# Nine buffers for the preparation of the right operands in a hybrid attention and gated-linear-attention block

## The chip, the cores and the metric

The kernel runs on one core of a Trainium2 chip. The core has a matrix engine (TensorE, PE in the profile; PEld are its weight loads), a vector engine (VectorE, DVE), a scalar engine (ScalarE, ACT), GpSimd (POOL) and SyncE (SP), which here issues every transfer of data. The engines run side by side. Each works through its own list of instructions in order and waits where an instruction needs a result that isn't there yet. Sixteen DMA engines move the data that SP's instructions ask for. The metric is the device time of one execution in microseconds.

## What is computed

One decoder layer over 2048 tokens of 1024 features, all in float32. The normalized input goes through one wide projection. A part of its columns feeds sliding-window attention (16 heads, window 128), another a gated linear attention (GLA, 4 heads, in chunks of 64 tokens). The outputs of both, each times its own gate, go through the output projection; a per-layer embedding, times a gate of the residual stream, is added.

```python
u = rmsnorm(h, norm_mix[i])
z = u @ w_in[i]                                   # 1024 x 5392
aq, ak, av, gq, gk, gv, g_low, za, zg = jnp.split(z, offsets, axis=-1)
...
y = jnp.concatenate([y_att * jax.nn.silu(za), y_gla * jax.nn.silu(zg)], axis=-1) @ w_out[i]
h = h + y                                         # w_out: 2048 x 1024
gate = jax.nn.sigmoid(rmsnorm(h, ple_norm[i]) @ w_ple_gate[i])   # 1024 x 1024
h = h + gate * (p[i] @ w_ple_proj[i])
```

## The kernel before

**Precision.** Every float32 operand of a large product is split into a rounded part (float32r) and the rest, and three products of these are added up (`gemm`, lines 85 to 87). The rounding is done by ACT, the subtraction that gives the rest by DVE or POOL.

**First phase.** The tokens are worked in two halves of eight tiles of 128. In each half come section A (keys, values and low-rank gates), then for each of the four GLA heads `v_block`, `qk_block`, `gla_prep` and `gla_tile`, and behind them the attention groups (`za_block`, `att_tile`). Results go to DRAM as yts (stores yts<-oy from attention, line 480, and yts<-oyg from GLA, line 587). In the first half `load_w` reads a piece of w_in into a buffer raw, splits it into wh and wl and stores both to DRAM (wd); in the second half it loads wh and wl from there.

**Second phase.** Three products of 1024 x 1024 matrices (the two halves of w_out, then w_ple_gate) are done in a seven-product scheme. Its right operands T0 to T6 are sums and differences of the blocks of the weight matrix, split as above. `products` uses them in the order ORDER = (0, 4, 1, 6, 5, 2, 3), for one or two pairs of token tiles at a time.

**Right operands.** They are prepared in the second half of the first phase by the generator `right_operands` in 48 pieces (3 matrices, 4 row blocks, 4 column blocks). A piece loads four 128 x 128 blocks of the weights (tile rb, line 605); DVE forms four differences of them (tile tm, `diff`, line 104); then, once for three blocks of rb and once for tm, ACT rounds into a tile th (line 620), POOL subtracts in place (line 621), and SP stores both parts to DRAM, td0 to td2 (line 623). These four tiles of a piece, and the raw pieces of `load_w`, share one pool, rawp, of three buffers of 2176 bytes per partition. `tick` advances the generator between the tiles of the main work; where it yields it gives its turn away. The loads of the next piece stand at the end of a piece.

**Order.** The program is built by a framework that schedules the instructions of each engine at build time and picks the buffer of each tile. So a yield sets when a piece is offered, and what stands where in an engine's list is seen in the order of the built program.

**Between the phases.** When the last group of the second half begins, the pool kvp (keys, values and attention scratch) is closed and T0 and T4 are loaded in its space (pool tpr, `load_T`, line 122). The other five are loaded when the first phase's pools are closed (pool tpb), behind the loads of the second phase's first left operands (y<-yts) and residuals (xt<-in_x).

Of the kernel before, what the change touches and what calls it, by code (L numbers as in the profile page):

```python
# [11 lines left out]
F32R = mybir.dt.float32r  # L12
# [7 lines left out]
P = 128  # L20
# [18 lines left out]
def hybrid_block_kernel(  # L39
# [5 lines left out]
    nc = tc.nc  # L45
# [44 lines left out]
    p2p = {}  # L90
# [12 lines left out]
    def diff(eng, o, i0, i1):  # L103
        eng.tensor_tensor(o, i0, i1, op=ALU.subtract)  # L104
# [9 lines left out]
    ORDER = (0, 4, 1, 6, 5, 2, 3)  # L114
    srcs = [w_out[0:D, :], w_out[D:2 * D, :], w_ple_gate]

    def load_T(ps_, which, T):
        for i in which:
            T[i] = p2p["tpr" if i in ORDER[:2] else "tpb"].tile(
                [P, 2, 4, 512], F32R, name=f"T{i}", tag="T", bufs=2 if i in ORDER[:2] else 5)  # L120
            for k in range(4):
                nc.sync.dma_start(T[i][:, :, k, :].bitcast(F32), tds[ps_][:, i, :, k, :])

# [2 lines left out]
    with ExitStack() as p1:  # L126
        kvs = p1.enter_context(ExitStack())
        kvp = kvs.enter_context(tc.tile_pool(name="kvp", bufs=1, side="right"))
        rawp = p1.enter_context(tc.tile_pool(name="rawp", bufs=3))
        wps = [p1.enter_context(tc.tile_pool(name=f"wp{i}", bufs=1)) for i in range(2)]  # L130
        up = p1.enter_context(tc.tile_pool(name="up", bufs=1))
        c1 = p1.enter_context(tc.tile_pool(name="c1", bufs=1))
# [175 lines left out]
        def tick():  # L308
            for c in list(chains):
                if next(c, True):  # L310
                    chains.remove(c)

        def spawn(c):
            chains.append(c)
# [12 lines left out]
        def u_norm(half, lt):  # L327
            t = half * HT + lt
            xt = u_load(half, lt)
            junk = w2("junk", BF16, (P, 1024))  # L330
            ss = small.tile([P, 1], F32, name="ss", tag="ss", bufs=4)
            act.activation(junk, xt, AF.Square, accum_out=ss)
            rs = rms_scale(ss, D)
            xts[t] = (xt, rs)

        def u_scale(half, lt):
            xt, rs = xts[half * HT + lt]
            for sl in ((slice(0, 512), slice(512, 1024)) if half + lt == 0 else (slice(0, 1024),)):
                dve.scalar_tensor_tensor(xt[:, sl], xt[:, sl], rs, nm[:, sl], op0=ALU.mult, op1=ALU.mult)
# [14 lines left out]
        def carry_kv():  # L354
            act.activation(kT[:, :, :, 0:P], kT[:, :, :, HT * P:(HT + 1) * P], AF.Copy)
            act.activation(vs[:, 0], vs[:, HT], AF.Copy)
# [232 lines left out]
        def run_chain(c):  # L589
            next(c)  # L590
            tick()
            spawn(c)


        def right_operands():
            units = [(ps_, k, c) for ps_ in range(3) for k in range(4) for c in range(4)]

            def piece(name, dtype=F32):
                return rawp.tile([P, 2 * SW], dtype, name=name, tag="raw")[:, 0:512].rearrange("p (b n) -> p b n", b=4)

            def load(ps_, k, c):
                r = piece("rb")

                for i, (kk, a) in enumerate(((0, 1), (0, 0), (1, 0), (1, 1))):
                    nc.sync.dma_start(r[:, i], srcs[ps_][(k + 4 * kk) * P:(k + 4 * kk + 1) * P,
                                                         512 * a + c * P:512 * a + c * P + P])
                return r

            r = load(*units[0])
            yield  # L610
            for n, (ps_, k, c) in enumerate(units):

                tm = piece("tm")
                diff(dve, tm[:, 1], r[:, 0], r[:, 1])
                diff(dve, tm[:, 2], r[:, 3], tm[:, 1])
                diff(dve, tm[:, 0], r[:, 2], tm[:, 2])
                diff(dve, tm[:, 3], r[:, 3], r[:, 0])
                for src, i0, m in ((r[:, 1:4], 0, 3), (tm, 3, 4)):
                    h = piece("th", F32R)[:, 0:m]
                    act.activation(h, src, AF.Copy)  # L620
                    pool.tensor_tensor(src.bitcast(F32R), src, h, op=ALU.subtract)  # L621
                    for j, part in enumerate((h.bitcast(F32), src)):
                        nc.sync.dma_start(tds[ps_][:, i0:i0 + m, j, k, c * P:(c + 1) * P], part)
                    if i0 == 0:
                        yield
                if n + 1 < len(units):
                    r = load(*units[n + 1])
                yield

        A_COLS = [(C_AK, 256), (C_GL, 16)]  # L630
        LAG = 1
# [14 lines left out]
        def qk_weights(i):  # L646
            return load_w([(C_GQ + 128 * i, 128), (C_GK + 128 * i, 128)])

        for half in range(2):
            if half > 0:  # L650
                carry_kv()
                spawn(right_operands())
            wv = load_w([(C_GV, 256)])
            vt, gates = {}, {}
            for s_ in range(HT + LAG):
                if half + s_ + 3 < HT:
                    u_norm(half, half + s_ + 3)
                    u_scale(half, half + s_ + 3)
                if half + s_ + 2 < HT:
                    u_tr(half, half + s_ + 2)  # L660
                if s_ < HT:
                    a = section_a(half, s_, wA)
                    next(a)
                    if half == 0 and s_ == 0:
                        constants()
                    tick()
                    spawn(a)
                if s_ == HT - 1:
                    wqk = qk_weights(0)
                if s_ == HT:  # L670
                    gla_gates(half, 0, 0, gates)
                if s_ >= LAG:
                    v_block(wv, vt, s_ - LAG)
                    tick()

            for i in range(4):
                if i > 0:
                    vt, gates = {}, {}
                    wv = load_w([(C_GV + 256 * i, 256)])
                    wqk = qk_weights(i)  # L680
                    for lt in range(HT):
                        if lt == 4:
                            gla_gates(half, i, 0, gates)
                        v_block(wv, vt, lt)
                        tick()
                if half == 1 and i == 3:

                    kvs.close()
                    p2p["tpr"] = p2r.enter_context(tc.tile_pool(name="tpr", bufs=1, side="right", reuse_waits="tile"))
                    T = [None] * 7  # L690
                    load_T(0, ORDER[:2], T)
                wz = load_w([(C_ZG + 256 * i, 256)])
                qks = {}
                def qk_sub(sub):
                    for j in range(2):
                        qk_block(wqk, qks, gates, sub, j)
                        tick()

                qk_sub(0)
                ops = {0: gla_prep(0, qks, vt)}  # L700
                for lt in range(HT):
                    if lt == 1:
                        gla_gates(half, i, 1, gates)
                    if lt == 3:
                        qk_sub(1)
                    c = gla_tile(half, i, wz, lt, ops)
                    next(c)
                    if lt < HT - 1:
                        ops[lt + 1] = gla_prep(lt + 1, qks, vt)
                    run_chain(c)  # L710
                    if half == 0 and i == 3:
                        if lt == 3:
                            wA = load_w(A_COLS)
                        if lt >= 4:
                            u_norm(1, lt - 4)
                            u_scale(1, lt - 4)
                        if lt >= 5:
                            u_tr(1, lt - 5)
                for g in ((0, 1), (2,), (3,), ())[i]:
                    wz = load_w([(C_ZA + 256 * g, 256)])  # L720
                    wq = load_w([(C_AQ + 256 * g, 256)])
                    szas = {}
                    for kind, j in (("z", 0), ("q", 0), ("q", 1), ("z", 1), ("q", 2), ("q", 3),
                                    ("q", 4), ("z", 2), ("q", 5), ("q", 6), ("z", 3), ("q", 7)):
                        if kind == "z":
                            za_block(wz, szas, j // 2, j % 2)
                            tick()
                        else:
                            run_chain(att_tile(half, g, wq, j, szas))
# [6 lines left out]
    with ExitStack() as p2:  # L736
        for name in ("xpb", "tpb", "fs"):
            p2p[name] = p2.enter_context(tc.tile_pool(name=name, bufs=1, reuse_waits="tile"))
        fs = p2p["fs"]
        load_T(0, ORDER[2:], T)  # L740


        def combos(As):
# [295 lines left out]
        for n, (ps_, prs) in enumerate(blocks):  # L1039
# [13 lines left out]
            Cs, qs, T = Csn, qsn, Tn  # L1053
# [27 lines left out]
```

## Time and profile before

| | |
|---|---|
| median of 3 runs | 1964.96 us (1962.47 to 1968.51) |
| profiled execution | 1964.2 us, span 1962.5 us |
| PE busy | 1836.1 us, 94% of the span |
| DVE, ACT, POOL busy | 62%, 49%, 35% |
| mean granted TensorE clock | 0.981 of full speed |
| moved by DMA | 326.8 MB, 167 GB/s over the span |

The busy shares are means over two unlike phases; what binds in a stretch is seen in the rows of that stretch.

### The profile page before, as it was taken

The numbers are of one execution on the slowest core, as the hardware profiler recorded it, in microseconds if no ns is written. First come the engines' busy times: TensorE is split into PE (matmuls) and PEld (weight loads), VectorE is DVE, ScalarE is ACT, GpSimd is POOL, SyncE is SP. The second block draws the span as 40 slices with busy tenths as digits, with TensorE's granted clock in tenths as the row PEclk, the third lists the DMA queues.
The fourth block names the chain that finished last, engine by engine and source line by source line (L and its number), as shares of the span: only waits on it lengthen the run. The fifth ranks groups of instructions, "written<-read, shape, count | busy, mean of one in ns | idle before, by whom it ended". The sixth has DMA issues, their size and how long they took to land.

```text
span 1962.5 us, 32888 instructions
## 1 busy us (share of the span) xinstructions
PE 1836.1 (94%) x11297; PEld 1628.0 (83%) x11297; DVE 1209.6 (62%) x2663; ACT 962.9 (49%) x2598; POOL 693.5 (35%) x916
## 2 busy tenths in 40 slices
PE   6999999999999888899897999999899999999997
PEld 6989898998988787887787888998778888787886
DVE  6455774574475664567764585475657666765865
ACT  5555674465465454345654465365422235453543
POOL 5452454454444564534534353222200001002432
PEclk9999999999999999999898999999999999999999
DMA  7332442433424656556565563334495876894542
GB/s 250 98 121 69 145 143 78 146 120 96 151 84 145 200 180 185 170 149 188 152 191 154 158 193 118 108 98 140 145 346 189 287 268 229 273 349 137 181 144 81
DMA packets 326743, 326.80 MB, mean 167 GB/s; under 512 B 23136, under 2 KB 259824, under 8 KB 326320
## 3 DMA queue, kind: packets, MB, share of 16 engines
q1 hardware_dynamic: 326576, 324.70, 51.9%
q8 instruction: 89, 1.46, 0.3%
q14 instruction: 78, 0.64, 0.1%
HBM read 186.08 MB, written 138.54 MB: 165 GB/s over the span
## 4 chain that ended last, share of the span: by engine, by line
PE 57%; DMA 17%; DVE 9%; ACT 7%; SPq 4%; issue 4%; POOL 2%; DVEq 0%; ACTq 0%; POOLq 0%
PE acc L85 9%; PE acc L86 9%; PE acc L87 9%; DMA rb<-in_w_out 3%; PE acc L765 3%; PE acc L766 3%; PE acc L767 3%; PE o L767 2%; PE o L766 2%; PE o L765 2%; DMA td<-th 2%; DMA td<-rb 2%; DMA wl<-wd 2%; DMA rb<-in_w_ple_gate 2%; DMA raw<-in_w_in 1%
## 5 line engine op out<-in xcount | busy, mean ns | idle before, releaser
L85 PE MATMUL acc<-wh,uth 128*128 128x256 f32 (+1 forms) x1664 | 480.1, 289 | 18.1 <-DVE m L563 7.7
L86 PE MATMUL acc<-wl,uth 128*128 128x256 f32 (+1 forms) x1664 | 476.0, 286 | 2.3 <-DMA wl<-wd 1.2
L87 PE MATMUL acc<-wh,utl 128*128 128x256 f32 (+1 forms) x1664 | 475.5, 286 | 0.0
L85 PEld LDWEIGHTS acc<-wh,uth 128*128 128x128 f32 x1664 | 319.4, 192 | 28.5 <-DVE m L563 9.1
L86 PEld LDWEIGHTS acc<-wl,uth 128*128 128x128 f32 x1664 | 319.5, 192 | 8.1 <-DMA wl<-wd 2.8
L87 PEld LDWEIGHTS acc<-wh,utl 128*128 128x128 f32 x1664 | 319.5, 192 | 2.1
L460 POOL TENSOR_TENSOR pq<-pq,pmask 128x512 fp32r<-128x512 f32 x128 | 174.4, 1376 | 292.0 <-ACT pq L67 277.7
L85 PE MATMUL acc<-uth,wh 128*128 128x512 f32 x512 | 205.4, 401 | 4.2 <-DVE m L563 3.2
L87 PE MATMUL acc<-uth,wl 128*128 128x512 f32 x512 | 202.6, 396 | 1.1 <-DMA wl<-wd 1.1
L86 PE MATMUL acc<-utl,wh 128*128 128x512 f32 x512 | 203.3, 397 | 0.0
L765 PE MATMUL acc<-T,c 128*128 128x512 f32 (+1 forms) x344 | 135.6, 395 | 9.3 <-DMA T<-td 6.8
L767 PE MATMUL acc<-T,c 128*128 128x512 f32 (+1 forms) x344 | 135.0, 392 | 0.0
L766 PE MATMUL acc<-T,c 128*128 128x512 f32 (+1 forms) x344 | 134.8, 392 | 0.0
L288 POOL TENSOR_TENSOR wl<-raw,wh 128x512 fp32r<-128x512 f32 (+1 forms) x82 | 110.0, 1361 | 51.8 <-ACT wh L286 37.1
L446 ACT ACTIVATE s<-s,sm 128x128 f32<-128x128 f32 x256 | 99.6, 390 | 44.2 <-DVE sm L442 43.4
L85 PEld LDWEIGHTS acc<-uth,wh 128*128 128x128 f32 x512 | 97.3, 190 | 26.4 <-DVE m L563 4.5
L850 POOL TENSOR_TENSOR ssh<-ssh 128x1 f32<-128x1 f32 x16 | 3.8, 238 | 318.3 <-ACT junk L849 318.3
L87 PEld LDWEIGHTS acc<-uth,wl 128*128 128x128 f32 x512 | 96.9, 189 | 23.4 <-DMA wl<-wd 1.5
L86 PEld LDWEIGHTS acc<-utl,wh 128*128 128x128 f32 x512 | 97.2, 190 | 19.3
L67 ACT ACTIVATE c<-s 128x512 fp32r<-128x512 f32 x72 | 45.1, 629 | 113.2 <-DVE s L104 29.8
L621 POOL TENSOR_TENSOR rb<-rb,th 128x384 fp32r<-128x384 f32 x48 | 50.5, 1053 | 139.8 <-DVE tm L104 90.6
L765 PE MATMUL o<-T,c 128*128 128x512 f32 (+1 forms) x252 | 99.6, 395 | 0.0
(288 smaller groups left out, 4478.8 us busy)
## 6 DMA issues: line engine op xcount, KB each, us to landing
T<-td SPq DMA_DIRECT2D x84, 512.0 KB, 9.3
wd<-wh SPq DMA_DIRECT2D x20, 1024.0 KB, 5.0
wd<-wl SPq DMA_DIRECT2D x20, 1024.0 KB, 6.6
wl<-wd SPq DMA_DIRECT2D x80, 256.0 KB, 5.6
wh<-wd SPq DMA_DIRECT2D x80, 256.0 KB, 5.4
raw<-in_w_in SPq DMA_DIRECT2D x68, 256.0 KB, 3.7
y<-yts SPq DMA_DIRECT2D x64, 256.0 KB, 6.0
td<-th SPq DMA_DIRECT2D x48, 256.0 KB, 2.5
```

Of the source, the lines that this page charges most:

```text
L67: act.activation(h, src, AF.Copy)
L85: pe.matmul(ps, lhs_h(k), rhs_h(k), start=(k == 0), stop=False)
L86: pe.matmul(ps, lhs_h(k), rhs_l(k), start=False, stop=False)
L87: pe.matmul(ps, lhs_l(k), rhs_h(k), start=False, stop=(k == nk - 1))
L288: eng.tensor_tensor(wl[:, ks_, 0:n], raw[:, :, 0:n], wh[:, ks_, 0:n], op=ALU.subtract)
L446: act.activation(s[:, j, :], s[:, j, :], AF.Exp, bias=ng[:, j:j + 1], accum_out=su[:, j:j + 1])
L460: pool.tensor_tensor(pq[:, 2 + i, :].rearrange("p (h n) -> p h n", h=4), pq[:, i, :].rearrange("p (h n) -> p h n", h=4), pmb, op=ALU.mult)
L621: pool.tensor_tensor(src.bitcast(F32R), src, h, op=ALU.subtract)
L765: pe.matmul(ps, c[:, 0, k, :], t[:, 0, k, sl], start=(first and k == 0), stop=False, skip_group_check=more)
L766: pe.matmul(ps, c[:, 0, k, :], t[:, 1, k, sl], start=False, stop=False, skip_group_check=more)
L767: pe.matmul(ps, c[:, 1, k, :], t[:, 0, k, sl], start=False, stop=(k == 3), skip_group_check=more)
L850: pool.tensor_tensor(ss[:, 0:1], ss[:, 0:1], ss[:, 1:2], op=ALU.add)
```

## The change

The pool rawp gets nine buffers instead of three and moves to the other side of the memory, beside kvp, with which it is closed. Its space comes from the scratch of the dynamic DMA, which is set to 1024 bytes. `right_operands` loads two pieces ahead instead of one and gives one more turn away in every third piece. The third operand in ORDER, T1, is loaded with T0 and T4, into a pool tpr of three buffers; tpb has four instead of five.

```diff
     def load_T(ps_, which, T):
         for i in which:
-            T[i] = p2p["tpr" if i in ORDER[:2] else "tpb"].tile(
-                [P, 2, 4, 512], F32R, name=f"T{i}", tag="T", bufs=2 if i in ORDER[:2] else 5)
+            T[i] = p2p["tpr" if i in ORDER[:3] else "tpb"].tile(
+                [P, 2, 4, 512], F32R, name=f"T{i}", tag="T", bufs=3 if i in ORDER[:3] else 4)
...
-        rawp = p1.enter_context(tc.tile_pool(name="rawp", bufs=3))
+        rawp = kvs.enter_context(tc.tile_pool(name="rawp", bufs=9, side="right"))
...
-            r = load(*units[0])
+            rs_ = [load(*u) for u in units[:2]]
             yield
             for n, (ps_, k, c) in enumerate(units):
+                r = rs_.pop(0)
...
-                if n + 1 < len(units):
-                    r = load(*units[n + 1])
+                if n + 2 < len(units):
+                    rs_.append(load(*units[n + 2]))
                 yield
+                if n % 3 == 0:
+                    yield
...
-                    load_T(0, ORDER[:2], T)
+                    load_T(0, ORDER[:3], T)
...
-        load_T(0, ORDER[2:], T)
+        load_T(0, ORDER[3:], T)
...
-    nc = _bacc.Bacc("TRN2", target_bir_lowering=False, num_devices=1)
+    nc = _bacc.Bacc("TRN2", target_bir_lowering=False, num_devices=1, dynamic_dma_scratch_size=1024)
```

What stands where changes on every engine. SP's list shows it best, since a piece's loads and stores are all in it. First the place where the pieces begin, near the end of the first half; yts_59 to yts_64 are the stores of the first half's last attention group, tiles 2 to 7. Before:

```order
L480 DMA yts_61<-oy 128x256
L480 DMA yts_62<-oy 128x256
L480 DMA yts_63<-oy 128x256
L284 DMA raw<-in_w_in 128x2x256
L605 DMA rb<-in_w_out 128x128
L480 DMA yts_64<-oy 128x256
L605 DMA rb<-in_w_out 128x128
```

And now:

```order
L605 DMA rb<-in_w_out 128x128 x3
L480 DMA yts_59<-oy 128x256
L292 DMA wd_7415<-wh 128x8x256
L605 DMA rb<-in_w_out 128x128 x5
L480 DMA yts_60<-oy 128x256
L292 DMA wd_7415<-wl 128x8x256
L624 DMA td_145<-th 128x3x128
L624 DMA td_145<-rb 128x3x128
```

The first loads moved from behind the store of tile 6 to ahead of that of tile 2, two pieces are loaded at once, and the first stores of a piece follow the store of tile 3.

Second the place where the pieces end; td_147 belongs to the last of the three matrices, yts_65 to yts_72 to the tiles of the second half. Before:

```order
L623 DMA td_147<-th 128x3x128
L623 DMA td_147<-rb 128x3x128
L480 DMA yts_72<-oy 128x256
L623 DMA td_147<-th 128x4x128
L623 DMA td_147<-tm 128x4x128
L587 DMA yts_65<-oyg 128x256
L587 DMA yts_66<-oyg 128x256
L278 DMA wh<-wd_6623 128x2x256
```

And now:

```order
L624 DMA td_147<-th 128x3x128
L624 DMA td_147<-th 128x4x128
L624 DMA td_147<-rb 128x3x128
L624 DMA td_147<-tm 128x4x128
L480 DMA yts_65<-oy 128x256
L278 DMA wh<-wd_2744 128x2x256
L480 DMA yts_66<-oy 128x256
L279 DMA wl<-wd_2744 128x2x256
```

Before, the last store of a piece stood between the last attention store of the third group and the stores of the third GLA head. Now it stands ahead of the first attention store of the whole second half. Between the first and the last of these transfers SP issues 466 transfers of 80.6 MB now, counted from the rows' shapes.

Third the place where T0 and T4 (the first two, from td_145) are loaded. Before:

```order
L122 DMA T_16789<-td_145 128x2x512 x4
L480 DMA yts_72<-oy 128x256
L122 DMA T_16794<-td_145 128x2x512 x4
L587 DMA yts_65<-oyg 128x256
L587 DMA yts_66<-oyg 128x256
```

And now:

```order
L122 DMA T_16790<-td_145 128x2x512 x4
L480 DMA yts_72<-oy 128x256
L122 DMA T_16795<-td_145 128x2x512 x4
L122 DMA T_16800<-td_145 128x2x512 x4
L587 DMA yts_65<-oyg 128x256
L587 DMA yts_66<-oyg 128x256
```

T1 (T_16800) stands behind T4 now; the burst behind the y and x loads begins with T6.

## Rows read from the trace of the kernel before

**Rows 1.** The page, part 1: busy time, share, instructions.

```profile
PE 1836.1 (94%) x11297; PEld 1628.0 (83%) x11297; DVE 1209.6 (62%) x2663; ACT 962.9 (49%) x2598; POOL 693.5 (35%) x916
```

**Rows 2.** Stretches: length, PE, PEld, DVE, ACT, POOL busy (instructions), clock, DMA share, GB/s.

```profile
100.00:555.00 455.00, 444.51 (x3078) 408.12 (x3077) 272.80 (x652) 252.11 (x753) 203.61 (x224) 1.00 0.36 114
577.00:880.00 303.00, 268.51 (x1832) 245.90 (x1831) 170.75 (x428) 148.99 (x416) 146.86 (x224) 0.96 0.59 175
620.00:1210.00 590.00, 524.96 (x3482) 474.11 (x3480) 354.87 (x913) 297.66 (x864) 270.10 (x346) 0.96 0.60 176
1210.00:1390.00 180.00, 178.68 (x1232) 163.62 (x1233) 100.30 (x252) 89.57 (x274) 51.36 (x78) 1.00 0.30 97
```

**Rows 3.** Waits of PE, 600 to 1220 us: total, times, longest.

```profile
PE o L525 <- ACT sh L67: 12.1, 6, 3.6
```

**Rows 4.** Waits of all engines, 600 to 1220 us.

```profile
DVE tm L104 <- DMA rb<-in_w_out: 55.5, 30, 5.7
...
ACT th L620 <- DMA rb<-in_w_out: 49.0, 19, 7.7
ACT th L620 <- DMA td<-th: 47.9, 25, 5.7
DVE tm L104 <- DMA rb<-in_w_ple_gate: 38.8, 23, 9.9
ACT th L620 <- DMA rb<-in_w_ple_gate: 35.4, 11, 11.7
```

**Rows 5.** A piece's instructions: all 48, DVE's and POOL's means, those of 577:880.

```profile
L620 ACT ACTIVATE th<-tm x48: 614/631/636, 629.2 to 1205.3; 128x512 fp32r<-128x512 f32 x48
...
L104 DVE TENSOR_TENSOR tm<-rb 128x128 f32<-128x128 f32 x96 | 32.6, 343 | 68.4 <-DMA rb<-in_w_ple_gate 29.7 <-DMA rb<-in_w_out 28.4 <-DMA td<-th 3.6
L104 DVE TENSOR_TENSOR tm<-rb,tm 128x128 f32<-128x128 f32 x96 | 30.1, 313 | 36.3 <-DMA rb<-in_w_out 27.1 <-DMA rb<-in_w_ple_gate 9.1
...
L621 POOL TENSOR_TENSOR tm<-tm,th 128x512 fp32r<-128x512 f32 x48 | 65.3, 1360 | 60.9 <-ACT th L620 59.9 <-PE t L346 0.7 <-DMA td<-rb 0.2
...
L621 POOL TENSOR_TENSOR rb<-rb,th 128x384 fp32r<-128x384 f32 x48 | 50.5, 1053 | 139.8 <-DVE tm L104 90.6
...
L620 ACT ACTIVATE th<-tm x21: 615/632/634, 629.2 to 871.3; 128x512 fp32r<-128x512 f32 x21
```

**Rows 6.** Timeline of PE around the first use of T1 (start, duration).

```profile
1425.85 0.77 PE L765 MATMUL acc<-T,c 128*128 128x512 f32 x1 [6.54 <-DMA T<-td]
...
1427.27 0.63 PE L765 MATMUL acc<-T,c 128*128 128x512 f32 x1
...
1433.31 0.39 PE L767 MATMUL acc<-T,c 128*128 128x512 f32 x1
1433.53 0.39 PE L765 MATMUL sw<-T,c 128*128 128x512 f32 x1
```

**Rows 7.** SP's attention stores, 570 to 900 and 850 to 900 us: count, ns, first and last.

```profile
L480 SPq DMA_DIRECT2D yts<-oy x8: 320/336/421, 577.6 to 886.5; - x8
...
L480 SPq DMA_DIRECT2D yts<-oy x2: 389/405/421, 879.8 to 886.5; - x2
```

**Rows 8.** Stretches with a high DMA share, columns as in rows 2.

```profile
1400.00:1440.00 40.00, 30.91 (x142) 24.51 (x141) 24.04 (x43) 14.06 (x33) 4.44 (x9) 0.91 0.96 332
...
680.00:700.00 20.00, 17.24 (x139) 16.42 (x138) 15.19 (x31) 11.38 (x31) 11.27 (x22) 1.00 0.86 269
...
640.00:700.00 60.00, 51.97 (x371) 47.59 (x372) 38.08 (x86) 29.99 (x88) 32.25 (x54) 1.00 0.73 219
```

**Rows 9.** Timeline of SP's queue: the loads of T between the phases.

```profile
1353.38 3.89 SPq L122 DMA_DIRECT2D T<-td  x4
1377.61 22.62 SPq L587 DMA_DIRECT2D yts<-oyg  x4
...
1417.94 23.39 SPq L122 DMA_DIRECT2D T<-td  x20
```

**Rows 10.** The first 60 us, columns as in rows 2.

```profile
0.00:60.00 60.00, 44.27 (x314) 42.02 (x314) 38.66 (x94) 33.17 (x77) 30.97 (x82) 0.97 0.64 206
```

## The prediction

> **What bounds the kernel now.** I read the page first: TensorE (PE) is busy 94% of the span [rows 1], so a gain has to come from the few places where it waits. A table of stretches finds them [rows 2]. The count behind PE's busy time is one of matmuls, and since the mix of matmuls hardly differs inside the first phase, matmuls per microsecond is a usable speed. From 100 to 555 us, before any right operand is prepared, PE issues 3078 in 455 us, 6.77 per us. From 1210 to 1390 us, when the last is done, 1232 in 180 us, 6.84 per us. Between, from 620 to 1210 us, 3482 in 590 us: at 6.77 that is 515 us of work, so **75 us are lost while right operands are prepared**. The granted clock is part of the loss (0.96 there, 1.00 before and after).
>
> The waits of PE there are short and come from ACT and DVE; the largest sum is 12.1 us, for a rounding on ACT [rows 3]. So the question is what ACT and DVE wait for. That is the next view [rows 4]: the differences on DVE (tm) waited 55.5 + 38.8 = 94 us for the loads of rb, and the roundings on ACT (th) waited 49.0 + 35.4 = 84 us for the same loads and 47.9 us for the landing of an earlier store of th. Engines work in order, so an evacuation that PE needs stands behind each such wait. The last is the sign of too few buffers: with three for the four tiles of a piece, the second th of a piece takes the buffer of the first, and the next rb that of this rb. A piece therefore carries a load and the landings of two stores one behind the other, and the 48 pieces, from 629 to 1205 us, come one per 12.3 us [rows 5].
>
> The other loss is at the start of the second phase: PE stops 6.54 us for T1 and then works at the lower clock (a matmul shows 0.63 us instead of 0.39), so that T1's 24 matmuls end only at 1433.5 [rows 6].
>
> **The change, part by part.**
>
> *Nine buffers, loads two pieces ahead.* No instruction is added or taken away; waits are. Nine buffers hold two pieces and a load, and a tile now takes a buffer that was last used about two pieces earlier. At most the 94 + 84 + 48 = 226 us of waits on DVE and ACT vanish, and with them at most the 75 us of PE. What is late next? The order shows that the scheduler uses the freedom to pack the pieces: they now begin ahead of the third attention store of the first half's last group and end ahead of the first attention store of the second half. In the trace of before these two stores are issued at 577.6 and 879.8 us [rows 7], so all 48 pieces share a stretch that held 21 [rows 5]. Without loss it holds 1832 matmuls / 6.77 = 271 us of PE work, against 303 us now [rows 2]. 27 more pieces come into it. A piece costs DVE 2 x 0.343 + 2 x 0.313 = 1.3 us and POOL 1.05 + 1.36 = 2.4 us [rows 5], so DVE goes from 171 to 206 us of 271 and POOL from 147 to 212: busy, not full.
>
> DMA is another matter. By the order's shapes SP issues 80.6 MB in this stretch (56.6 MB of pieces, 24 MB of weights, x and results). In the stretch as it is, 175 GB/s made a share of 0.59, so the engines move 175 / 0.59 = 297 GB/s when all are busy with this mix; 80.6 MB are 271 us of all 16 engines: as long as PE's own work. So the stretch can't fall to 271 us unless the DMA engines never rest. From both sides: over 1400 to 1440 us they reached a share of 0.96, with rows of 2 KB (512 columns) where the pieces have 512 bytes (128 columns); the best 20 us of the present mix is 0.86; the densest 60 us hold 0.73 [rows 8]. At 0.96 the stretch takes 283 us (12 lost), at 0.86 316 us (45 lost), at 0.73 371 us (100 lost). I take 0.86, the highest that this mix has shown: 45 lost. What follows has no pieces left and, like 1210 to 1390, loses nothing. **Gain 75 - 45 = 30 us.**
>
> The Trainium skill (DMA: Bandwidth & Descriptors, Where 436 GB/s comes from) puts the limit for transfers to and from HBM at about 358 GB/s for a core. By that figure 80.6 MB would be an estimated 225 us, the DMA would not bind, and the whole 75 us could be had. The trace of this mix gives 297, and the sum goes by the trace.
>
> *The extra turn given away in every third piece* would spread the pieces, but the order shows them denser all the same: nothing.
>
> *Space out of the DMA scratch.* The code issues every transfer on nc.sync, and nothing else in it would use that scratch. Nothing. The pieces' buffers move to the right side of the memory, which only matters for T1.
>
> *T1 early.* Four loads of 512 KB move from the burst at 1418 us to behind those of T4, issued from 1353.4 to 1357.3 us [rows 9], where SP issues nothing else until 1377.6. T1 is then there when PE comes to it, at 1425.85 - 6.54 = 1419.3 us. Its 24 matmuls, 0.23 us apart at full clock (1433.31 to 1433.53 in the rows), take 5.5 us, to 1424.8. Now T6 heads the burst and lands when T1 did, at 1425.8: a wait of 1.0 us. T6's products begin at 1425.8 instead of 1433.5: **7.7 us, taken as 7**. Twenty loads took 23.4 us, 4.7 us a T [rows 9], and PE uses 5.5 us for each with two pairs, so no later T is waited for. Bounds: 0, if T6 is as late for PE as T1 was, and 9.
>
> *The first 60 us.* Nine buffers also let weight loads run ahead: five of them now stand ahead of the fourth x tile on SP. PE idles 15.7 us of these 60 [rows 10]. Weights sooner, x later: taken as 0, and as bounds a third of that idle time each way, 5 us. The rest of the first half runs at 6.77 per us and offers next to nothing.
>
> Sum, against the profiled execution's own 1964.2 us (span 1962.5; the median of the runs, 1964.96, is 0.8 higher): 1964.2 - 30 - 7 = **1927 us**.
>
> **The rivals.**
> 1. *The loss is all but hidden.* The DMA keeps 0.96, as at 1400 to 1440 us: 75 - 12 + 7 = 70 us, **1894**. For it: at 271 / 48 = 5.6 us a piece, loads two pieces ahead and buffers two pieces back leave each transfer some 11 us to land. Against: the short rows of the pieces, and POOL and DVE close to 80%. The Trainium skill's figure above (DMA: Bandwidth & Descriptors) speaks for this rival, with an estimated 1964.2 - 75 - 7 = 1882 us at its end.
> 2. *The waits move, the loss stays.* PE is held up not by the waits but by the pieces' work standing in DVE's and ACT's queues; packed closer, the same work costs the same 75 us. Only T1 counts: **1957**. For it: PE's waits sum to little beside the 226 us on DVE and ACT, so most of those were already harmless. Against: 12 us a piece and the waits' names.
> 3. *Slower: the DMA engines choke.* 0.77 is the point: there the stretch takes 271 / 0.77 = 352 us, the 75 + 7 us are spent. At 0.73, the densest 60 us so far, it takes 371 us: 1964.2 + 25 - 7 = **1982**. Weights that PE needs stand on the same SP queue behind the pieces. Against: those 60 us were limited by demand, the buffers' chain, as far as rows 4 show.
>
> **How the numbers follow.** My forecast (1910 to 1945) gets 0.50, rival 1 (below 1910) 0.20, rival 2 (1945 to 1966) 0.18, rival 3 0.12. A measurement of this kernel tells about 0.3% from no change: 1959 and 1971 are the borders. Faster: 0.50 + 0.20 and most of rival 2, 0.80; same 0.09; slower 0.11. For 8 in 10 the range reaches into rivals 1 and 2: 1888 to 1963.
>
> **What would show it.** Right: DVE's waits for rb fall from 94 us to under 20 and ACT's for a store of th from 48 to under 10; the last td store goes out near 890 us instead of after 1205; the DMA share over the packed stretch is 0.8 or more; behind it PE runs at 6.8 matmuls per us; no wait for T1 and at most 2 us for T6. Wrong: if DVE or ACT wait in the packed stretch for stores (td) or PE for weights (wh, wl) by tens of microseconds, the transfers have become the bound (rival 3); if those waits are gone and PE still loses 70 us to DVE and ACT, it is the work itself (rival 2). A stretch that ends before 865 us would mean that 297 GB/s was no limit (rival 1).

## The result and the profile after

The median fell from 1964.93 to **1931.09 us** (1929.69 to 1938.03); the ratio is 0.9833, with a 95% interval of 0.9805 to 0.9861. 1927 us were predicted. The profiled execution has a span of 1927.6 us, 34.9 less than before.

The page of the kernel after, busy time, answers to [rows 1]:

```profile
PE 1828.3 (95%) x11297; PEld 1626.3 (84%) x11297; DVE 1224.1 (64%) x2663; ACT 962.7 (50%) x2598; POOL 697.9 (36%) x916
```

Its stretches, columns as in [rows 2]:

```profile
0.00:60.00 60.00, 43.04 (x282) 40.36 (x283) 36.86 (x93) 33.32 (x76) 29.66 (x78) 0.91 0.71 232
577.00:900.00 323.00, 281.32 (x1846) 254.90 (x1845) 225.49 (x534) 178.58 (x473) 215.81 (x279) 0.93 0.89 259
620.00:1210.00 590.00, 549.61 (x3677) 499.08 (x3676) 379.63 (x935) 311.42 (x898) 278.21 (x360) 0.97 0.58 171
900.00:1390.00 490.00, 483.51 (x3327) 441.73 (x3326) 296.06 (x729) 253.03 (x780) 142.30 (x181) 1.00 0.32 102
```

From 620 to 1210 us PE issues 3677 matmuls instead of 3482 [rows 2]. At 6.77 per us that is 590 - 3677 / 6.77 = 46.9 us lost instead of 75.7. All of it lies in the packed stretch, 577 to 900 us: 323 - 1846 / 6.77 = 50 us. Behind it PE runs at 6.8 per us, and nothing is lost.

Of these 50 us some 15 are longer matmuls, at a granted clock of 0.93 (152 ns of busy time for each, 144 from 100 to 555 us [rows 2]); the rest is idle time of PE. PE's waits in this stretch are short and all for DVE and ACT, which write its operands and empty its results (evacuations); none is for a load. The two largest sums of 577 to 900 us:

```profile
PE acc L85 <- DVE m L563: 7.1, 4, 3.2
PE o L526 <- DVE sh L68: 3.8, 3, 2.2
```

The stores of the pieces end where the order had said, at 898 us, and not behind 1205 [rows 5]. SP's queue, the kernel after, duration min/median/max, then first and last:

```profile
L624 SPq DMA_DIRECT2D td<-tm x48: 359/391/1887, 596.8 to 897.9; - x48
```

The waits of 600 to 1220 us, which answer to [rows 4]:

```profile
DVE tm L104 <- DMA rb<-in_w_out: 21.4, 14, 5.9
...
ACT th L621 <- DMA rb<-in_w_out: 16.9, 10, 3.2
ACT th L621 <- DVE tm L104: 16.7, 15, 3.6
...
ACT th L621 <- DMA td<-th: 12.2, 5, 8.6
POOL rb L622 <- DVE tm L104: 11.8, 9, 3.0
...
ACT th L621 <- DMA rb<-in_w_ple_gate: 8.4, 6, 2.1
...
DVE tm L104 <- DMA rb<-in_w_ple_gate: 6.6, 4, 3.7
```

The five waits of [rows 4] were 226 us; they are 65.5 now.

Between the phases, PE of the kernel after (T1's first products, T6's first is the sw):

```profile
1394.31 0.80 PE L768 MATMUL acc<-T,c 128*128 128x512 f32 x1 [4.84 <-ACT u L823]
1394.90 0.63 PE L769 MATMUL acc<-T,c 128*128 128x512 f32 x1
...
1402.38 0.39 PE L768 MATMUL sw<-T,c 128*128 128x512 f32 x1
```

The wait for T1 is gone [rows 6]; in its place PE waits 4.84 us for a copy u on ACT, and works at the lower clock behind it as before (0.50 granted from 1394 to 1398 us, a matmul shows 0.63 us).

### The profile page after: what moved, and what is told of

It is laid out like the page before. It is cut to its first block, busy times and chain, and to the rows that moved or that the text cites. A ratio compares the mean times of both kernels' runs of the same rounds, so it can differ in the third digit from the quotient of the medians.

```text
span 1927.6 us, 32806 instructions
## 1 busy us (share of the span) xinstructions
PE 1828.3 (95%) x11297; PEld 1626.3 (84%) x11297; DVE 1224.1 (64%) x2663; ACT 962.7 (50%) x2598; POOL 697.9 (36%) x916
## 5 line engine op out<-in xcount | busy, mean ns | idle before, releaser
L446 ACT ACTIVATE s<-s,sm 128x128 f32<-128x128 f32 x256 | 99.7, 391 | 51.6 <-DVE sm L442 51.3
L87 PEld LDWEIGHTS acc<-uth,wl 128*128 128x128 f32 x512 | 97.2, 190 | 23.8 <-DMA wl<-wd 1.7
L288 POOL TENSOR_TENSOR wl<-raw,wh 128x512 fp32r<-128x512 f32 (+1 forms) x82 | 109.9, 1370 | 20.2 <-ACT wh L286 10.3
L768 PE MATMUL o<-T,c 128*128 128x512 f32 (+1 forms) x252 | 98.7, 392 | 1.1 <-DVE xt L107 0.9
L769 PE MATMUL o<-T,c 128*128 128x512 f32 (+1 forms) x252 | 98.0, 389 | 0.0
L770 PE MATMUL o<-T,c 128*128 128x512 f32 (+1 forms) x252 | 97.9, 389 | 0.0
```

Of the source, the lines that this page charges most:

```text
L87: pe.matmul(ps, lhs_l(k), rhs_h(k), start=False, stop=(k == nk - 1))
L288: eng.tensor_tensor(wl[:, ks_, 0:n], raw[:, :, 0:n], wh[:, ks_, 0:n], op=ALU.subtract)
L446: act.activation(s[:, j, :], s[:, j, :], AF.Exp, bias=ng[:, j:j + 1], accum_out=su[:, j:j + 1])
L768: pe.matmul(ps, c[:, 0, k, :], t[:, 0, k, sl], start=(first and k == 0), stop=False, skip_group_check=more)
L769: pe.matmul(ps, c[:, 0, k, :], t[:, 1, k, sl], start=False, stop=False, skip_group_check=more)
L770: pe.matmul(ps, c[:, 1, k, :], t[:, 0, k, sl], start=False, stop=(k == 3), skip_group_check=more)
```

## The experiments

Two marks serve for all of them: the time of the first product of T0 in the profile (1405.5 us before, 1376.9 after), and the us lost from 620 to 1210, by matmuls at 6.77 per us. How far they can be trusted is seen in e4, whose PE list is that of after up to T1: 1381.1 and 51.6. So differences of some 5 us in the marks say nothing. The ratio is to executions of the kernel before that were taken beside each run.

| kernel | us, median | ratio to before (95%) | first T0 | lost 620:1210 |
|---|---|---|---|---|
| before | 1964.93 | | 1405.5 | 75.7 |
| after | 1931.09 | 0.9833 (0.9805 to 0.9861) | 1376.9 | 46.9 |
| e1 loads held back | 1904.35 | 0.9688 (0.9667 to 0.9708) | 1352.1 | 22.9 |
| e2 half the bytes | 1985.36 | 1.0092 (1.0067 to 1.0117) | 1371.9 | 40.5 |
| e3 later splits | 1938.66 | 0.9854 (0.9831 to 0.9877) | 1378.7 | 48.6 |
| e4 T1 late | 1938.12 | 0.9861 (0.9840 to 0.9883) | 1381.1 | 51.6 |
| e5 no subtractions | 1928.61 | 0.9806 (0.9791 to 0.9821) | 1374.7 | 44.2 |
| e6 no differences | 1933.69 | 0.9835 (0.9819 to 0.9851) | 1381.2 | 54.8 |
| e7 subtractions on DVE | 1937.56 | 0.9845 (0.9830 to 0.9860) | 1381.8 | 54.0 |
| e8 held, begun early | 1929.15 | 0.9807 (0.9792 to 0.9822) | 1380.1 | 24.9 |
| e9 compute held back | 1910.60 | 0.9706 (0.9681 to 0.9731) | 1354.5 | 23.1 |
| e10 half bytes, no subtractions | 1971.90 | 1.0021 (1.0002 to 1.0040) | 1357.2 | 23.8 |
| e11 one piece ahead | 1944.75 | 0.9877 (0.9850 to 0.9905) | 1386.3 | 57.5 |
| e12 held by the producer | 1904.40 | 0.9682 (0.9659 to 0.9706) | 1351.4 | 21.5 |

**e1, spread the pieces.**

```diff
                 r = piece("rb")
+                pool.tensor_copy(r[0:1, 0, 0:1], recent[0][0:1, 0, 0:1])
```

`recent` holds the oy or oyg that was made last ahead of this place in the program.

> The kernel after the change, with each piece's loads held until the latest attention or GLA result ahead of them in the program is there (one element of it is copied into the piece's buffer by POOL before the loads overwrite it). The order then spreads the 48 pieces from about 720 to 1260 us instead of 578 to 898. Theory (bytes per microsecond of DMA bound the packed stretch): spread out, the DMA share stays under 0.7, the nine buffers keep the waits away, and of the 50 us lost in 577 to 900 at most 15 are left: 1885 to 1900 us. Rival (the pieces' work in the queues of ACT, DVE and POOL costs PE the same wherever it stands): 50 us or more are lost in the new stretch too, 1925 to 1955 us.

27 us faster than after, and 4 over the theory's range. Windows of e1:

```profile
577.00:900.00 323.00, 307.61 (x2163) 282.24 (x2162) 212.48 (x511) 177.71 (x513) 161.72 (x254) 0.99 0.56 170
620.00:1210.00 590.00, 560.67 (x3839) 512.65 (x3838) 384.96 (x973) 317.35 (x932) 286.42 (x425) 0.98 0.59 176
```

The same work, the same bytes in 620 to 1210 (DMA share 0.59, 0.60 before [rows 2]), and 53 us less lost than before. From 577 to 900 us PE is idle for 15.4 us instead of 41.7. The rival, that the work costs the same wherever it stands, falls. But spreading thins out everything at once, bytes and work, so this doesn't show that bytes were the bound. e2 tests that.

**e2, half the bytes.**

```diff
-                        nc.sync.dma_start(tds[ps_][:, i0:i0 + m, j, k, c * P:(c + 1) * P], part)
+                        nc.sync.dma_start(tds[ps_][0:64, i0:i0 + m, j, k, c * P:(c + 1) * P], part[0:64])
```

> The kernel after the change, storing only half of each prepared right operand (partitions 0 to 63) and reading that half twice, so the output is not the reference's; no compute instruction is changed. The packed stretch moves 58.6 MB instead of 80.6. Theory (DMA bound): at 297 GB/s that is 197 us of all engines, well under PE's 271, so the loss in the stretch falls from 50 us to under 20: 1895 to 1905 us. Rival (the pieces' work itself): the engines do the same work, the loss stays at 45 us or more: 1925 to 1932 us.

The total rises in the second phase, where T is loaded in halves: these loads are 24% of the chain of work that ended last from 1400 us on, and PE's two longest stops, 27 us each, are for tiles xt, whose transfers share SP's queue with them. The stretch is what counts. Windows of e2:

```profile
577.00:900.00 323.00, 284.60 (x1905) 259.81 (x1905) 234.10 (x545) 183.16 (x492) 207.23 (x274) 0.94 0.70 185
```

The DMA share fell from 0.89 to 0.70, and still 323 - 1905 / 6.77 = 42 us are lost of 50. T0's first product comes 5 us earlier, no more than the marks scatter. The pieces even end later, at 929.3 us. **The theory falls:** with the DMA free for 30% of the time, its rate is not what holds this stretch.

What e2 did not lighten is SP's list. It has as many transfers as that of the kernel after, and a store of half the partitions takes SP longer, 575 ns in e2 against 391 in the kernel after:

```profile
L625 SPq DMA_DIRECT2D td<-tm x48: 574/575/690, 597.7 to 929.3; - x48
```

By the medians of these transfers, the pieces' loads and stores take SP an estimated 170 us in the kernel after and 195 in e2. So SP's issuing as a link isn't ruled out.

**e5, e6, e7: the engines' work one by one.** e5 leaves out the first line below, e6 the four differences (blocks are loaded a second time instead), e7 moves the subtraction.

```diff
-                    pool.tensor_tensor(src.bitcast(F32R), src, h, op=ALU.subtract)
+                    dve.tensor_tensor(src.bitcast(F32R), src, h, op=ALU.subtract)
```

> The kernel after the change without POOL's two subtractions in a piece (the low part is stored unsubtracted, so the output is not the reference's). Loads, stores, ACT's and DVE's work stay. Theory (POOL's 116 us of subtractions, packed into 300 us, delay POOL's other work and lengthen DVE's instructions with two operands in SBUF: 760 instead of 533 ns for a 128x256 one): most of the 50 us lost in 577 to 900 goes, 1890 to 1905 us. Rival (the loss comes from ACT's and DVE's instructions of the pieces): at most 15 us go, 1917 to 1931 us.

> The kernel after the change without DVE's four differences in a piece; four blocks of the weights are loaded a second time in their place, so the output is not the reference's and 12.6 MB more are moved. POOL's and ACT's work stay. Theory (POOL is what costs): the 63 us of DVE's own work are worth little, 1915 to 1931 us. Rival (DVE's queue is what costs PE): 25 us or more go, 1885 to 1906 us.

> The kernel after the change with the pieces' two subtractions moved from POOL to DVE; the result is the same. POOL loses 116 us of work, DVE gains some 50 to 60. Theory (POOL's share is what costs, through its queue and through DVE's longer instructions): 10 to 25 us faster than after, 1906 to 1921 us. Rival (DVE's queue is what costs): slower, 1935 to 1960 us.

None moves the time by more than the intervals overlap: e5 0.9806, e6 0.9835, e7 0.9845 against 0.9833. Neither POOL's 116 us nor DVE's 63 us is by itself what costs, as far as these runs show: e6 also loads more, and its pieces end only at 1041 us, so that it changes their spacing too. e7's 1937.6 lies in its rival's range, but by the ratio it is not told from after. No run takes work off ACT. POOL's part in DVE's durations is real nevertheless. DVE's instructions of the kernel after, 580 to 895 us (vv has two operands in SBUF; m has one there, acc is in PSUM):

```profile
L68 DVE TENSOR_TENSOR vv<-v,vv 128x256 fp32r<-128x256 f32 x16 | 12.1, 760 | 1.9 <-ACT vv L67 1.9
L563 DVE SCALAR_TENSOR_TENSOR m<-m,acc 128x256 f32<-128x256 f32 x16 | 6.6, 413 | 8.6 <-ACT m L562 8.4
```

The same lines in e5, same stretch:

```profile
L68 DVE TENSOR_TENSOR vv<-v,vv 128x256 fp32r<-128x256 f32 x16 | 7.6, 478 | 1.9 <-ACT vv L67 1.9
L563 DVE SCALAR_TENSOR_TENSOR m<-m,acc 128x256 f32<-128x256 f32 x16 | 6.7, 416 | 11.0 <-ACT m L562 10.9
```

vv takes 760 ns beside the subtractions and 478 without them; m is the same. But the time that e5 gives DVE back does not reach PE. The waits of e5, 600 to 1220 us, show where it goes:

```profile
ACT th L621 <- DMA rb<-in_w_out: 36.5, 15, 11.0
DVE tm L104 <- DMA rb<-in_w_out: 32.5, 21, 6.4
...
ACT th L621 <- DMA rb<-in_w_ple_gate: 24.8, 13, 3.8
...
DVE tm L104 <- DMA rb<-in_w_ple_gate: 20.6, 16, 3.8
```

With POOL out of the way ACT and DVE stand 114 us before loads, 53 in the kernel after. In e2 it is the other way round. Its waits, same stretch:

```profile
POOL rb L623 <- DVE tm L104: 35.3, 17, 8.6
...
ACT th L622 <- DVE tm L104: 28.9, 24, 3.2
...
ACT th L622 <- DMA rb<-in_w_out: 20.7, 11, 7.8
...
DVE tm L104 <- DMA rb<-in_w_out: 10.8, 11, 2.5
```

ACT and DVE wait 39 us for loads there (with 4.0 and 3.2 for w_ple_gate), but the engines wait longer for each other: 35 and 29 us instead of 11.8 and 16.7. That suggested a chain of links of like strength, and a test of it.

**e10, two links at once**: the edits of e2 and of e5 (half bytes and no subtractions) together.

> Half the bytes of the prepared operands and no subtractions on POOL, both at once (the output is not the reference's). The first product of the second phase came at 1376.9 us in the kernel after the change, at 1371.9 with half the bytes alone and at 1374.7 without the subtractions alone. If each resource costs for itself, the two add up: about 1370 us. Theory (the pieces are a chain, and where one link is made lighter the waits move to the next): more than the sum, 1345 to 1362 us. The second phase is slower by the reading of half tiles and is not compared.

PE of e10:

```profile
1357.16 0.50 PE L768 MATMUL acc<-T,c 128*128 128x512 f32 x1
```

1357.2, where 1370 was the sum of the single effects: 19.7 us for both, 5.0 and 2.2 for each alone. The loss from 620 to 1210 says the same, 23.1 against 6.4 and 2.7. By the marks the excess is 12 to 14 us, but each mark is of one execution, and the one of e2 took 3 us more than its median. The ratios, from all executions, say less: without the subtractions e2 gets 0.0071 faster (14 us, the intervals of e2 and e10 lie apart), the kernel after 0.0027 (5 us, the intervals overlap). The excess is then 9 us, with an uncertainty about as large. So it is shown that the subtractions cost 14 us where the bytes are halved; that the two links together are worth more than their sum is likely, not shown.

**e11, loads one piece ahead** (`units[:1]`, `n + 1`), all else as after.

> The kernel after the change with the loads one piece ahead as before the change, nine buffers kept. The order ends the pieces a little later (ahead of the 14th instead of the first attention store of the second half). By the theory that density costs, about the same or a little faster, 1922 to 1932 us; by the theory that waits for loads cost, slower, 1935 to 1950.

9 us slower than after by the ratios (whose intervals overlap a little), 9 and 11 by the two marks. Its waits, 600 to 1220 us:

```profile
DVE tm L104 <- DMA rb<-in_w_out: 62.0, 41, 5.8
ACT th L621 <- DMA rb<-in_w_out: 48.4, 23, 8.2
...
ACT th L621 <- DMA rb<-in_w_ple_gate: 16.4, 10, 3.2
...
DVE tm L104 <- DMA rb<-in_w_ple_gate: 7.4, 6, 3.3
```

134 us before loads instead of 53. Waits cost here, then, though the pieces are less densely packed (their last store goes out at 1021.9 us). By this some 9 of the change's 34 us are the loads two pieces ahead. The sum of such waits is no measure of PE's loss, though: e5 has 61 us more of them than after and loses no more. And no run has the other parts of the change without the nine buffers, so that what the buffers alone give is inferred from what is left over.

**e9, hold the compute, not the loads.** The one-element copy now goes into tm and th.

```diff
                 tm = piece("tm")
+                hold(tm[0:1, 1, 0:1])
...
+                    if i0 == 0:
+                        hold(h[0:1, 0, 0:1])
```

> The kernel after the change with the pieces' compute held instead of their loads: the first difference (DVE) and the first rounding (ACT) of a piece wait until the latest attention or GLA result ahead of them in the program is there; a one-element copy on the engine that made this result carries the wait. The loads are free to run ahead as far as the nine buffers allow. All the work and all the bytes stay. Theory (what costs PE is that ACT and DVE stand in order in front of a piece whose data are not there yet): with loads long landed the waits of ACT and DVE for rb fall under 10 us in all, and the time is at or under that of the paced kernel, 1890 to 1905 us. Rival (the paced kernel gained because its loads were spread, not its work): with loads bunched again 1915 us or more.

1910.6 us: 20 faster than after, and 5 over the range. But the loads did not bunch again. A buffer stays taken until its piece is worked, and so the loads spread with the compute. SP's loads of e9:

```profile
L615 SPq DMA_DIRECT2D rb<-in_w_out x128: 328/484/1501, 577.7 to 1028.8; - x128
L615 SPq DMA_DIRECT2D rb<-in_w_ple_gate x64: 328/485/917, 1043.1 to 1217.6; - x64
```

In e1 they go from 579.3 to 1215.9, and the DMA share from 577 to 900 us is 0.56 there and 0.55 here. So e9 repeats e1's gain by another hold; whether the spread of the loads or that of the compute gives it, this run can't tell, and its rival stands untested. Loads are not quite waited away: DVE and ACT stand 10.5 and 9.6 us before rb, where under 10 in all was expected.

**e8, begun in the first half** (e1 with the generator spawned at the third GLA head of the first half).

> The paced kernel (each piece's loads held until the latest attention or GLA result ahead of them in the program), with the generator started in the first half ahead of its third GLA head, so that the 48 pieces are spread over some 390 to 1150 us instead of 720 to 1260. Theory (the loss grows with how densely the pieces' work stands): less than the paced kernel's 1904 us, 1885 to 1900. Rival (the rest of the paced kernel's loss does not come from density, or the first half has no room beside its own splits of w_in): 1904 us or more.

The rival holds. Windows of e8:

```profile
340.00:560.00 220.00, 206.17 (x1378) 188.44 (x1377) 133.71 (x299) 113.19 (x326) 114.94 (x138) 0.96 0.50 154
```

The kernel after issues 1519 matmuls from 340 to 560 us, e8 1378: 141 / 6.77 = 21 us go there, where POOL, DVE and ACT also split the pieces of w_in. Spreading into that time gave nothing here.

**e12, who holds.** As e1, with the copy made by the engine that makes the result.

> The paced kernel, with the one-element copy that holds a piece's loads made by the engine that makes the result it waits for (DVE for attention, ACT for GLA) instead of POOL. In the paced kernel POOL stands 17 us before such copies for attention results and 13 us for GLA results, with its subtractions behind it. Theory (an engine that stands in order in front of a result that is not there yet holds up the work of PE behind it): a few us faster than the paced kernel, 1896 to 1902 us. Rival (POOL's waits reach PE nowhere): 1902 to 1907 us.

0.9682 against 0.9688: the same. POOL's 30 us before these copies have no effect on the time that could be told.

**e4, T1 late again** (the two ORDER[:3] are ORDER[:2]).

> The kernel after the change with T1 loaded late again, as before the change; nothing else differs. By the prediction's step T1 is worth 7 us: 1938 us. By the traces (PE waited 6.54 us for T1 before, 4.84 us for ACT's copy now) it is worth 2 to 3: 1933 to 1934 us.

PE of e4, T1's first product:

```profile
1402.16 0.77 PE L768 MATMUL acc<-T,c 128*128 128x512 f32 x1 [8.34 <-DMA T<-td]
```

The ratio is 0.0028 above that of after, 5.5 us, but the intervals overlap, and 4.2 us of it lie ahead of T0's first product, where the lists are the same. From T0's first product to T6's the profiles have 28.7 us in e4, 28.0 before and 25.5 after: T1 early is worth 3 us.

**e3, the copy u freed.** The splits of the last three left operands of the first block are written behind the product of T4.

> The kernel after the change, where the splits of the first block's last three left operands are written behind the product of T4, so that ACT's copy of product 0, for which PE waits 4.84 us at the start of T1, no longer stands behind them. Theory (this copy is the second wait, hidden until now behind T1's landing): the wait of 4.84 us and the half clock behind it go, 5 to 7 us faster than after: 1924 to 1926 us. Rival (T1 itself or T6 lands too late for more): the wait only changes its name, 1930 to 1932 us.

Not faster by the runs; from T0's first product to T6's its profile has 23.5 us instead of 25.5. ACT of e3:

```profile
1393.85 0.63 ACT L67 ACTIVATE c<-y 128x512 fp32r<-128x512 f32 x1 [4.23 <-DMA y<-yts]
1394.39 1.07 ACT L833 ACTIVATE u<-acc 128x512 f32<-128x512 f32 x2
```

The splits are gone from ahead of u, and another split stands there instead, which waits 4.23 us for a y of the load burst between the phases. PE still waits 3.31 us for u. So the second wait behind T1 is shown, but the cause that I had given it was not the last one.

## Why the prediction came out

The time was right, 1927 against 1931.1; one of its mechanisms was not. That the sum came so close was partly luck: the 45 us had the wrong reason, and the 4 us too many for T1 are made up by 3.7 that came where nothing was expected.

- **75 us are lost while right operands are prepared, through the waits for loads and buffers.** Right in the direction. The five waits fell from 226 to 65.5 us and 28.8 us of the loss with them; e11 brings back 81 us of the waits for loads and about 9 us of time. Two signs that were to show it were missed: DVE's waits for rb are 28 us, not under 20, and ACT's for a store of th 12.2, not under 10.
- **The pieces are packed from 577.6 to 879.8 us.** Right by the order; the first store goes out at 591, the last at 898, 18 us later than was put.
- **45 us are lost there, because the DMA holds a share of 0.86.** The size was right (50 us, at a share of 0.89), *the reason was the step that failed*. I took the share for the bound because bytes divided by the best rate gave a length near PE's own. e2 took the share to 0.70 and the loss stayed at 42 us. Rival 2's picture, that the pieces' work stands in the way, was nearer, but as I put it ("the same work costs the same 75 us" packed closer) e1 refutes it. What the runs show in its place: the loss depends on how closely the pieces stand, and neither halved bytes, nor POOL's subtractions taken out, nor DVE's differences replaced changes it by more than some 8 us by the marks, whose scatter is some 5. My account of it is argued, not shown: a piece is a chain of load, differences, rounding, subtraction and store over SP's DMA, DVE, ACT and POOL, and each engine works in order, so that a piece's instruction that stands before its data holds up the evacuations behind it. One link made lighter moves the waits to the next (e2, e5); with two, some 20 us come back by the marks (e10); with room for the chain, some 24 do (e1, e9). ACT's and SP's links were not lightened by any run.
- **What the kernel before shows beside this:** there the 48 pieces were spread over 576 us, in e1 over 524 (roundings from 696.0 to 1219.8), and 75.7 us were lost instead of 22.9. So spread alone isn't it; with three buffers and loads one piece ahead the chain waits however wide it stands.
- **Behind the pieces nothing is lost.** Right: 900 to 1390 us at 6.8 per us.
- **T1: 7 us.** The mis-sized term: 3. The timeline ended the wait with T1's landing, and the copy u, which PE needs for the same products, ended 2.9 us earlier, at 1422.9 (first row below), and was hidden by it. Only T1's release was read, not when the next thing was ready. The 4.7 us a T, too, were a misreading: 23.4 us is what SP took to issue the twenty loads. At 387 GB/s (second row) a T of 2.1 MB takes 5.4 us to land, just as long as PE uses it. No T was waited for all the same, neither T1 nor T6 nor a later one.
- **The first 60 us: 0, within 5.** PE issues 282 matmuls there instead of 314 [rows 10], 32 / 6.77 = 5 us behind; by the GLA results that follow it is 2 (the first head's last is copied out at 156 instead of 154 us). A loss at the edge of the bound.
- **Left over:** T0's first product came 28.6 us earlier and T6's 31.2; the span is 34.9 shorter. The 3.7 us that came in the second phase behind T6 were not predicted. They may be scatter: the profiles of e8 and e9, with the same second phase, have 523.3 and 529.6 us behind T6, before 529.0 and after 525.2.
- **The Trainium skill's limit** (DMA: Bandwidth & Descriptors, Where 436 GB/s comes from), 358 GB/s, which spoke for rival 1, would have left the DMA out of it. On the bound that was right, though not by its figure: at a share of 0.89 the stretch moved 259 GB/s, 291 at full share. And with rows of 2 KB the kernel before went past that limit, at 387 GB/s (second row below); there page and measurement differ, and the measurement decides.

The rows of the kernel before, ACT's copy u and a stretch of the T loads (columns as in [rows 2]; a share over 1 tells how rough the shares are):

```profile
1421.88 1.06 ACT L820 ACTIVATE u<-acc 128x512 f32<-128x512 f32 x2
...
1428.00:1438.00 10.00, 9.73 (x38) 7.55 (x38) 3.95 (x6) 1.90 (x3) 0.00 (x0) 0.88 1.05 387
```

What stays open is where the last 21 to 23 us of e1 and e12 go; in e1 one wait of PE for wh, 4.69 us, is among them. What the packed stretch costs on ACT and on SP was not tested, nor whether pieces spread still wider within the second half would give more.

## What to carry to other kernels

A sum that fits is no proof of its mechanism: a busy share near 0.9 says that a resource is used, and only a run that lightens it alone says whether it binds. Where background work is a chain over several in-order engines, look at its spacing first, since work taken off one engine may only move the waits to the next, and a scheduler that packs such work as early as the buffers allow may give away a good part of what the buffers gain; here holding back each piece's loads gave 27 us on top of the change's 34. When a wait is taken away, read what else the waiting instruction needs and when that was ready.

## What was not expected of the hardware

DVE's own instructions grow beside POOL's: vv of 128 x 256 takes 533 ns in 900 to 1300 us, 760 in the packed stretch, 478 there without POOL's subtractions, while m, with one operand in PSUM, stays at 413 to 416. The Trainium skill (SBUF — State Buffer, Who interferes with whom) says that a DVE instruction with two inputs in SBUF contends with a GpSimd instruction that reads SBUF, and that one with at most one such input, outside the modes that use both of DVE's ports, does not. The trace agrees with both halves. It had no effect on the time here that could be told (e5).
